# Moving the Fourier branch's gate projection beside attention in a two-layer hybrid block

## The chip, the cores and the metric

One Trainium2 chip, one core. The time is device microseconds (us) of one launch, taken as the median of the runs. The engines are TensorE (PE in the profile; PEld is its weight load), VectorE (DVE), ScalarE (ACT), GpSimd (POOL) and SyncE (SP), which issues all the transfers here. Each engine works through its own instructions in order.

## The reference

Two layers. Each normalises and modulates 1,024 latent tokens of width 1,024 (and in layer 0 a 256-token context prefix too), multiplies them by one wide matrix, and splits the columns over three branches, each multiplied by a SiLU gate before the output projection:

```python
hx = rms_norm(x, norm_g[l]) * (1.0 + scale[:, None, :]) + shift[:, None, :]
px = split_cols(hx @ w_in[l])         # q, k, v, g_att, c_a, c_b, g_conv, f_u, g_four
attn = windowed_attention(q, k, v, kc, vc, attn_sink[l])       # +-128 tokens, and the context
y_conv = conformer_conv(c_a, c_b, conv_w, conv_b, ln_g, ln_b)  # GLU, 31 taps, LayerNorm, swish
y_four = fourier_mix(f_u, w_four, b_four)                      # real part of a 2-D DFT, linear
y = jnp.concatenate([attn * silu(g_att), y_conv * silu(g_conv), y_four * silu(g_four)], -1)
x = x + gate[:, None, :] * (y @ w_out[l])
```

## The kernel before, in words

All is float32. Every large product is split into a high and a low part and done as three matmuls (`mm3`, lines 195 to 197). The unit of the work is a **block**: 128 columns of `w_in` against one chunk of tokens (`project`). A chunk is 512 latent tokens (128x512 matmuls) or the 256 context tokens (128x256); a block has 8 steps of depth, so 24 matmuls. The weights of the next 128 columns come by one transfer (`w_begin`, line 430) and are split into `wh` on ScalarE and `wl` on VectorE, or on GpSimd once attention runs (`split`, lines 404 and 405).

A layer has these stages:

1. The Fourier input columns, then the first GLU columns.
2. The list `todo` of column groups, which the generator `projections` walks block by block: the GLU columns (`C_A`, `C_B + P`, `C_A + P`), the Fourier gate (`C_GF`, two groups), keys, values, four groups of queries. In layer 0 a group is three blocks, in the last layer two, but three for keys and values. Between two blocks the loop takes one step of the generator `side`: the Fourier transform (`fourier`), then the output gate's sums (`gate_sums`, whose weight tiles are named `wada`, and whose last row is a small transfer from `b_ada` into the tile `gsum`), and in layer 0 the modulation of the next layer (`ada1`), four rounds of four 512 KB `wada` tiles in the same four buffers. A round's matmuls (line 285) read the buffers, and then the next round's transfers may be issued (line 276).
3. Attention: a pipeline of **steps**, four per 128 queries, 40 in layer 0 and 32 in the last. A step issues scores (lines 893, 895; tile `score`), transposes of the probabilities (949; `pt<-ident,p`) and products with the values (963; `mm<-ph,v` and `mm<-pl,v`), and after these **one block** of other work as filler: first the attention gate (`C_GATT`), then the convolution's gate (`C_GC`), then halves of the output projection (`Out.half`, also 24 matmuls), of which a tile of 128 tokens can have its two once its attention is done, stored to `od` and loaded again. A step without a filler has only its own matmuls.
4. The output halves that are left.

The depthwise convolution runs on VectorE: 31 **taps** per 128 channels and chunk group (`cy<-cu,cw,cy`), put into the queue `back` by `conv_taps` and taken out by `fill_v(us)`, some microseconds' worth per block by the table `budget`. The class `Behind` makes each wait, in the order of the program, behind VectorE's last instruction of other work. A scheduler then sets every engine's order at build time, by priority (the place in the program, lower first) and its own picture of time.

The Fourier gate's block ends with three operations: tanh on ScalarE, the gate `t<-t` on VectorE and the product with the branch `F<-F,t` on VectorE, and a store to `yd`:

```python
def g():
    V.scalar_tensor_tensor(out=th, in0=th, scalar=1.0, in1=o, op0=ALU.add, op1=ALU.mult)
def h():
    V.scalar_tensor_tensor(out=d, in0=d, scalar=scale, in1=th, op0=ALU.mult, op1=ALU.mult)
    nc.sync.dma_start(out=store[:, c0:c1], in_=d)
```

While attention runs, `g` is held to the start of the next step and `h` to its end.

Of the kernel before, what the change touches and what calls it, by code (L numbers as in the profile page):

```python
# [139 lines left out]
def tile_backbone(ctx: ExitStack, tc: tile.TileContext, a, out):  # L140
# [31 lines left out]

    def fill_v(us):
        V.background = True
        while back and us > 0:
            t, f = back.popleft()
            f()
            us -= t
        V.background = False


# [363 lines left out]
    def conv_taps(l, ct, u, z, spans):  # L545
# [7 lines left out]
        def tap(s0, s1, j):  # L553
# [3 lines left out]
                                   in1=z.cols(o0, o1), op0=ALU.mult, op1=ALU.add)  # L557
        for s0, s1 in spans:
            us = 1.25 if s0 == 0 else 0.4
            back.append((us, lambda a=(s0, s1): first(*a)))  # L560
            for j in range(KC):
                if j != 15:
                    back.append((us, lambda a=(s0, s1, j): tap(*a)))
        back.append((0.0, u.put))

# [601 lines left out]
    def drain(g):  # L1167
        for _ in g:
            pass
# [111 lines left out]
    for l in range(DEPTH):  # L1281
# [39 lines left out]
        def side():  # L1321

            yield from four
            tab.extend(bufs.get("rope") for _ in range(2))
            for i, name in enumerate(("k_cos", "k_sin")):
                nc.sync.dma_start(out=tab[i].lat, in_=a[name])
            gsum = bufs.get("gsum")
# [42 lines left out]
        def gf_evac(m):  # L1370
            def f(o, c0, c1):
                drain(four)
                gate_mul(F[m], 0.5, yd[256 + m * P:256 + (m + 1) * P, :])(o, c0, c1)
            return f, lambda: F[m].put()
# [3 lines left out]
        def values():  # L1378
# [5 lines left out]
            for g in range(0, NT, 4):  # L1384
# [18 lines left out]
                (C_A + P, full, glu_a(1, wctx), lambda: taps(1), mmx)]  # L1403
        for m in range(2):
            todo.append((C_GF + m * P, full) + gf_evac(m) + (mmx,))
        k_at = sum(len(t[1]) for t in todo) + 3
# [4 lines left out]
        q_at = sum(len(t[1]) for t in todo)  # L1411
        budget = [(3.0 if t[0] < C_V else 5.0) * (0.5 if c == 2 else 1.0) for t in todo for c in t[1]]
        for j in range(4):
# [3 lines left out]
        for i in range(q_at):  # L1417
            c = next(pj)
            steps(sd)
            if i >= k_at:  # L1420
                steps(kp)
# [20 lines left out]
        def rest():  # L1442
# [3 lines left out]
            for i, c in enumerate(pj):  # L1446
                if i == 4 * len(full) - 2:
                    raw = w_begin(l, C_GC)
                if i == 4 * len(full) - 1:
                    box.append(w_split(raw))  # L1450
# [201 lines left out]
```

## Time and profile before

| | |
|---|---|
| median of 3 runs | 1203.3 us (1202.12 to 1205.43) |
| the profiled execution | 1202.68 us, of which the span is 1200.6 us |
| TensorE busy | 1103.3 us (92%) |
| VectorE busy | 820.6 us (68%) |
| ScalarE, GpSimd busy | 554.7 us, 295.0 us |
| mean granted TensorE clock | 0.964 of 2.4 GHz |
| chain that ended last | PE 70%, DVE 10%, DMA 9%, ACT 4% |

The span is first to last instruction of the profiled execution; 2.1 us of its time lie around it. A view by windows adds up, for a stretch of the span, each engine's busy time and the number of its instructions, and gives the granted clock as a share of 2.4 GHz: 1.00 is all of the stretch at the upper level, 0.50 all of it at 1.2 GHz. The timeline gives an instruction's start, its duration, engine, line, output and inputs, and in brackets the idle time before it and what ended that. Matmuls overlap in it, so that a matmul's cost in a row of them is the distance between two starts.

### The profile page before, as it was taken

What the parts mean: (1) busy time and instruction counts of PE and PEld (TensorE: products, weight loads), DVE (VectorE), ACT (ScalarE), POOL (GpSimd) and SP (SyncE); (2) the same over time, 40 slices, a digit from 0 to 9 for tenths busy, and PEclk for the clock granted to TensorE, in tenths of its full rate; (3) what the DMA queues carried; (4) which work ended last, traced back from release to release, by engine and by line L of the source; (5) the groups of instructions that cost most, each with busy time, mean ns of one, the idle gap of its engine ahead of it and who ended that gap; (6) DMA issues with size and microseconds to landing.
All of it is one profiled execution on the core that took longest, in us unless ns stands there. A gap on an engine that the chain in (4) does not pass through costs nothing.

```text
span 1200.6 us, 17131 instructions
## 1 busy us (share of the span) xinstructions
PE 1103.3 (92%) x6165; PEld 925.9 (77%) x6165; DVE 820.6 (68%) x1665; ACT 554.7 (46%) x1209; POOL 295.0 (25%) x266
## 2 busy tenths in 40 slices
PE   5799999999999989999889999999989979988866
PEld 3488887888888878888668788788778868877754
DVE  3425879999577786666755369889656786766654
ACT  5563222312566655564646652222255654545541
POOL 1212000000222443544342120000022453334321
PEclk9799999999999999999979999999989989999889
DMA  9602273744332433544436423532243453322221
GB/s 332 218 25 71 70 239 113 225 137 108 84 97 75 149 115 102 166 142 132 115 120 227 145 65 116 184 110 79 88 93 106 136 145 103 110 74 71 71 71 53
DMA packets 154093, 146.49 MB, mean 122 GB/s; under 512 B 7398, under 2 KB 131734, under 8 KB 154008
## 3 DMA queue, kind: packets, MB, share of 16 engines
q1 hardware_dynamic: 154008, 145.40, 39.5%
q8 instruction: 49, 0.80, 0.3%
q14 instruction: 36, 0.29, 0.1%
HBM read 110.49 MB, written 34.87 MB: 121 GB/s over the span
## 4 chain that ended last, share of the span: by engine, by line
PE 70%; DVE 10%; DMA 9%; ACT 4%; issue 3%; SPq 2%; POOL 1%; DVEq 0%; ACTq 0%; POOLq 0%
PE mm L195 13%; PE mm L197 13%; PE mm L196 13%; PE pt L195 5%; PE pt L196 5%; PE pt L197 5%; PE mm L963 4%; PE pt L949 4%; DMA od<-ot 3%; PE score L893 2%; DVE score L57 2%; DVE pl L57 2%; PE score L895 2%; DMA wr<-od 1%; ACT p L919 1%
## 5 line engine op out<-in xcount | busy, mean ns | idle before, releaser
L195 PE MATMUL mm<-hxh,wh 128*128 128x512 f32 (+1 forms) x808 | 311.5, 386 | 5.5 <-DVE t L57 3.2
L197 PE MATMUL mm<-hxh,wl 128*128 128x512 f32 (+1 forms) x808 | 306.7, 380 | 2.4 <-POOL wl L405 2.3
L196 PE MATMUL mm<-hxl,wh 128*128 128x512 f32 (+1 forms) x808 | 307.4, 380 | 0.0
L195 PEld LDWEIGHTS mm<-hxh,wh 128*128 128x128 f32 x808 | 153.8, 190 | 37.5 <-DVE t L57 4.3
L57 DVE SCALAR_TENSOR_TENSOR cy<-cu,cw,cy 128x1014 f32<-128x1014 f32 (+20 forms) x180 | 180.1, 1007 | 2.6
L197 PEld LDWEIGHTS mm<-hxh,wl 128*128 128x128 f32 x808 | 153.6, 190 | 30.3 <-POOL wl L405 3.1
L935 POOL TENSOR_SCALAR p<-p,st 128x640 f32<-128x640 f32 (+2 forms) x144 | 114.4, 809 | 249.1 <-DVE st L57 129.1
L196 PEld LDWEIGHTS mm<-hxl,wh 128*128 128x128 f32 x808 | 154.0, 191 | 25.0 <-issue 0.5
L405 POOL TENSOR_TENSOR wl<-wr,wh 128x1024 fp32r<-128x1024 f32 x26 | 64.2, 2468 | 396.3 <-ACT wh L404 394.1
L954 ACT ACTIVATE ph<-pt 128x512 fp32r<-128x512 f32 x184 | 97.4, 542 | 121.0 <-PE pt L949 118.2
L57 DVE TENSOR_TENSOR pl<-pt,ph 128x512 fp32r<-128x512 f32 x184 | 112.3, 616 | 57.8 <-ACT ph L954 56.4
L949 PE MATMUL pt<-ident,p 128*128 128x128 f32 x640 | 107.6, 286 | 24.5 <-DVE pl L57 19.1
L919 ACT ACTIVATE p<-score,st 128x640 f32<-128x640 f32 (+2 forms) x144 | 105.3, 734 | 36.5 <-DVE st L57 29.2
L57 DVE CUSTOM_DVE_ANT_0 score<-score,mask,nsink 128x640 f32<-128x640 f32 (+2 forms) x144 | 110.8, 782 | 13.8 <-PE score L895 13.0
L195 PE MATMUL pt<-hxh,wh 128*128 128x512 f32 (+1 forms) x296 | 112.2, 383 | 3.9 <-ACT hxh L393 2.5
L404 ACT ACTIVATE wh<-wr 128x1024 fp32r<-128x1024 f32 x56 | 59.7, 1066 | 116.5 <-PE mm L196 73.1
L196 PE MATMUL pt<-hxl,wh 128*128 128x512 f32 (+1 forms) x296 | 111.1, 376 | 0.7 <-DVE hxl L57 0.7
L197 PE MATMUL pt<-hxh,wl 128*128 128x512 f32 (+1 forms) x296 | 110.4, 373 | 0.9 <-DVE wl L57 0.9
L949 PEld LDWEIGHTS pt<-ident,p 128*128 128x128 f32 x640 | 79.8, 146 | 38.2 <-POOL p L935 8.7
L963 PE MATMUL mm<-ph,v 128*128 128x256 f32 x320 | 93.1, 314 | 13.2 <-ACT ph L954 10.7
L963 PE MATMUL mm<-pl,v 128*128 128x256 f32 x320 | 93.7, 315 | 5.3 <-DVE pl L57 4.9
L963 PEld LDWEIGHTS mm<-ph,v 128*128 128x128 f32 x320 | 64.6, 202 | 18.3 <-ACT ph L954 15.8
(220 smaller groups left out, 1797.8 us busy)
## 6 DMA issues: line engine op xcount, KB each, us to landing
wada<-w_ada SPq DMA_DIRECT2D x48, 512.0 KB, 7.0
wr<-w_in SPq DMA_DIRECT2D x38, 512.0 KB, 4.1
qq<-qd SPq DMA_DIRECT2D x36, 256.0 KB, 4.3
x1d<-x SPq DMA_DIRECT2D x10, 512.0 KB, 3.0
xnd<-xr SPq DMA_DIRECT2D x10, 512.0 KB, 3.7
p<-xnd SPq DMA_DIRECT2D x10, 512.0 KB, 4.8
sg<-sgd SPq DMA_DIRECT2D x36, 128.0 KB, 3.0
od<-ot SPq DMA_DIRECT2D x18, 256.0 KB, 2.5
```

Source lines behind the costliest of these rows:

```text
L57: r = f(*args, **kw)
L195: T.matmul(o, lhsT=lhs[0], rhs=rhs[0], start=start, stop=False)
L196: T.matmul(o, lhsT=lhs[0], rhs=rhs[1], start=False, stop=False)
L197: T.matmul(o, lhsT=lhs[1], rhs=rhs[0], start=False, stop=stop)
L404: S.activation(hi, raw, AF.Copy)
L405: (E or (G if holding[0] else V)).tensor_tensor(out=lo, in0=raw, in1=f32(hi), op=ALU.subtract)
L893: T.matmul(sc[:, c0:512], lhsT=q2[:, h, :], rhs=kx[:, k0:k0 + nl], start=fst, stop=not fst)
L919: S.activation(pp[:, j * n:(j + 1) * n], z["sc"][j][:, 768 - n:768], AF.Exp, scale=-1.0, bias=st[:, j:j + 1], accum_out=st[:, 4 + j:5 + j])
L935: G.tensor_scalar(out=pp[:, j * n:(j + 1) * n], in0=pp[:, j * n:(j + 1) * n], scalar1=st[:, 6 + j:7 + j], scalar2=1.0, op0=ALU.mult, op1=A ...
L949: T.transpose(out=bt[:, (j % 2 * 2 + y) * P:(j % 2 * 2 + y + 1) * P], in_=pp[:, c0:c0 + P], identity=ident)
L954: S.activation(ph, bt[:, :w], AF.Copy)
L963: T.matmul(o, lhsT=self.vv[kt][:, kv * P:(kv + 1) * P], rhs=y.cols(j * 256, (j + 1) * 256), start=(j == 0 and x == 0), stop=(j == z["nkt"] ...
```

## The change

The Fourier gate's two column groups leave their place ahead of the keys and become the first fillers of attention (`q_at`, the number of blocks ahead of attention, falls by 6 in layer 0 and by 4 in the last). Their accumulators come from the two `mm` banks. What depended on the old place follows: the cosine and sine tables are loaded at the third block rather than behind the Fourier transform, `side` takes two steps per block from the first key block on, `budget` has 4 and 6 us instead of 3 and 5, and the convolution gate's weights are fetched two groups later. The taps get a priority later by 300, and the context's are put into the queue ahead of the latent's.

```diff
     def fill_v(us):
+        p0 = tc.cur_priority
+        tc.cur_priority = p0 + 300
         V.background = True
...
         V.background = False
+        tc.cur_priority = p0
...
-        for s0, s1 in spans:
+        for s0, s1 in spans[::-1]:
...
-        back.append((0.0, u.put))
+            back.append((0.0, u.put_ctx if s0 else u.put_lat))
...
             yield from four
-            tab.extend(bufs.get("rope") for _ in range(2))
-            for i, name in enumerate(("k_cos", "k_sin")):
-                nc.sync.dma_start(out=tab[i].lat, in_=a[name])
             gsum = bufs.get("gsum")
...
             def f(o, c0, c1):
-                drain(four)
                 gate_mul(F[m], 0.5, yd[256 + m * P:256 + (m + 1) * P, :])(o, c0, c1)
...
-        for m in range(2):
-            todo.append((C_GF + m * P, full) + gf_evac(m) + (mmx,))
         k_at = sum(len(t[1]) for t in todo) + 3
...
-        budget = [(3.0 if t[0] < C_V else 5.0) * (0.5 if c == 2 else 1.0) for t in todo for c in t[1]]
+        budget = [(4.0 if t[0] < C_V else 6.0) * (0.5 if c == 2 else 1.0) for t in todo for c in t[1]]
+        for m in range(2):
+            todo.append((C_GF + m * P, full) + gf_evac(m) + (mm,))
         for j in range(4):
             todo.append((C_GATT + j * P, full, gate_evac(sgd[j * P:(j + 1) * P, :]), None, mm))
...
             c = next(pj)
+            if i == 2:
+                tab.extend(bufs.get("rope") for _ in range(2))
+                for t, name in zip(tab, ("k_cos", "k_sin")):
+                    nc.sync.dma_start(out=t.lat, in_=a[name])
             steps(sd)
+            if i >= k_at - 3:
+                steps(sd)
             if i >= k_at:
...
-                if i == 4 * len(full) - 2:
+                if i == 6 * len(full) - 2:
                     raw = w_begin(l, C_GC)
-                if i == 4 * len(full) - 1:
+                if i == 6 * len(full) - 1:
                     box.append(w_split(raw))
```

Lines behind the first edit are 3 higher in the changed kernel (195 to 197 are 198 to 200). Three places of the built order:

**SP's queue, layer 0, ahead of attention**: the transfers of the last two rounds of `ada1` before (a round is four `wada` tiles; `wr` are weights of a column group, `qd<-q` stores queries).

```order
L276 DMA wada_1857<-w_ada 128x4x256
L276 DMA wada_1858<-w_ada 128x4x256
L276 DMA wada_1855<-w_ada 128x4x256
L276 DMA wada_1856<-w_ada 128x4x256
L430 DMA wr<-w_in 128x8x128
L1346 DMA qd_858<-q_150_2083 128x512
L276 DMA wada_1857<-w_ada 128x4x256
L276 DMA wada_1858<-w_ada 128x4x256
L276 DMA wada_1855<-w_ada 128x4x256
L276 DMA wada_1856<-w_ada 128x4x256
```

And now:

```order
L433 DMA wr<-w_in 128x8x128
L279 DMA wada_1738<-w_ada 128x4x256
L279 DMA wada_1739<-w_ada 128x4x256
L279 DMA wada_1736<-w_ada 128x4x256
L279 DMA wada_1737<-w_ada 128x4x256
L1346 DMA qd_858<-q_150_1878 128x512
L279 DMA wada_1738<-w_ada 128x4x256
L279 DMA wada_1739<-w_ada 128x4x256
L279 DMA wada_1736<-w_ada 128x4x256
L279 DMA wada_1737<-w_ada 128x4x256
L1346 DMA qd_858<-q_150_1878 128x512
```

The rounds stand closer: on TensorE the matmuls of one round and of the next had two blocks or three between them before, and have one now, which for the last round is a context block.

**VectorE's queue, layer 0, at the split `wl` of the first query group's weights** (`kr` is the key's rotation, `cy` the convolution's sums, of `cu` and the weights `cw`). Before, such a split stood so:

```order
L57 TENSOR_TENSOR kr_1762<-kr_1762,t_1811 128x512
L57 SCALAR_TENSOR_TENSOR cy_1352<-cu_1253,cw,cy_1352 128x1013
L57 SCALAR_TENSOR_TENSOR cy_1001<-cu_896,cw,cy_1001 128x243
L57 TENSOR_TENSOR wl<-wr,wh 128x1024
L57 SCALAR_TENSOR_TENSOR cy_1352<-cu_1253,cw,cy_1352 128x1014
```

And now:

```order
L57 SCALAR_TENSOR_TENSOR cy_1384<-cu_1283,cw,cy_1384 128x255 x2
L57 SCALAR_TENSOR_TENSOR cy_1384<-cu_1283,cw,cy_1384 128x254
L57 SCALAR_TENSOR_TENSOR cy_1384<-cu_1283,cw,cy_1384 128x253
L57 SCALAR_TENSOR_TENSOR cy_1384<-cu_1283,cw,cy_1384 128x252
L57 SCALAR_TENSOR_TENSOR cy_1384<-cu_1283,cw,cy_1384 128x251
L57 SCALAR_TENSOR_TENSOR cy_1384<-cu_1283,cw,cy_1384 128x250
L57 SCALAR_TENSOR_TENSOR cy_1384<-cu_1283,cw,cy_1384 128x249
L57 SCALAR_TENSOR_TENSOR cy_1384<-cu_1283,cw,cy_1384 128x248
L57 SCALAR_TENSOR_TENSOR cy_1384<-cu_1283,cw,cy_1384 128x247
L57 SCALAR_TENSOR_TENSOR cy_1384<-cu_1283,cw,cy_1384 128x246
L57 TENSOR_TENSOR wl<-wr,wh 128x1024
```

A run of 17 context taps now stands ahead of this split. In all, every tap of both layers still stands ahead of VectorE's third operation on attention scores.

**TensorE's queue, last layer, late in attention**. Before, a step had no filler between its two groups of scores and its products:

```order
L893 MATMUL score<-kh_7639,q_528_9846 128x384
L893 MATMUL score<-kd_7637,q_528_9846 128x384
L895 MATMUL score<-kh_7640,q_528_9846 128x256
L895 MATMUL score<-kd_7638,q_528_9846 128x256
L949 MATMUL pt<-ident,p_9952 128x128 x4
L963 MATMUL mm<-pl_9971,v_7873 128x256
L893 MATMUL score<-kh_7639,q_528_9846 128x384
L893 MATMUL score<-kd_7637,q_528_9846 128x384
```

The step before this one in the changed kernel's order ends with matmuls of an output half between the transposes and the next scores:

```order
L952 MATMUL pt<-ident,p_9730 128x128 x2
L198 MATMUL mm<-hxh_6194,wh 128x512
L199 MATMUL mm<-hxl_6196,wh 128x512
L200 MATMUL mm<-hxh_6194,wl 128x512
L198 MATMUL mm<-hxh_6198,wh 128x512
L199 MATMUL mm<-hxl_6200,wh 128x512
L200 MATMUL mm<-hxh_6198,wl 128x512
L896 MATMUL score<-kh_7447,q_528_9692 128x384
```

Of the last layer's 13 steps ahead of its last one, 6 had a block in the order before and 10 have one now; the order of the first 18 steps holds 15 blocks in both, and behind the last scores there are 4 in both. In layer 0 each of the last nine pairs or single steps of attention has at least one block now, where several had none.

## Rows read from the trace of the kernel before

**Rows 1.** The page: busy time of each engine, share of the span, instructions.
```profile
PE 1103.3 (92%) x6165; PEld 925.9 (77%) x6165; DVE 820.6 (68%) x1665; ACT 554.7 (46%) x1209; POOL 295.0 (25%) x266
```

**Rows 2.** Windows by stage: length, busy PE, PEld, DVE, ACT, POOL, clock, DMA, GB/s.
```profile
118.70:302.30 183.60, 183.60 (x1099) 150.86 (x1098) 164.66 (x251) 45.85 (x87) 2.95 (x1) 1.00 0.49 149
540.40:617.30 76.90, 70.64 (x383) 59.89 (x382) 49.35 (x149) 39.20 (x108) 32.73 (x36) 0.93 0.38 119
617.30:690.00 72.70, 65.79 (x310) 53.62 (x309) 34.39 (x85) 46.26 (x100) 20.77 (x21) 0.91 0.53 180
720.00:861.30 141.30, 141.24 (x709) 114.24 (x707) 119.84 (x141) 34.45 (x60) 0.15 (x1) 1.00 0.36 114
957.50:1008.00 50.50, 39.88 (x217) 34.70 (x216) 36.79 (x68) 24.48 (x55) 23.25 (x18) 0.93 0.50 144
1008.00:1043.90 35.90, 35.90 (x210) 31.63 (x209) 24.84 (x64) 18.41 (x45) 13.85 (x13) 1.00 0.29 96
1043.90:1149.10 105.20, 88.96 (x504) 76.33 (x502) 71.11 (x178) 58.23 (x139) 39.02 (x34) 0.94 0.25 70
```

**Rows 3.** Windows, line 195 alone (8 matmuls per block): PE, PEld.
```profile
540.40:617.30 76.90, 22.46 (x56) 10.66 (x56) 0.93 0.38 119
1008.00:1043.90 35.90, 12.63 (x32) 6.01 (x32) 1.00 0.29 96
1043.90:1149.10 105.20, 20.61 (x48) 9.76 (x48) 0.94 0.25 70
```

**Rows 4.** Timeline of PE: starts inside a latent block, then inside a context block.
```profile
299.65 0.39 PE L195 MATMUL mm<-hxh,wh 128*128 128x512 f32 x1
300.33 0.39 PE L195 MATMUL mm<-hxh,wh 128*128 128x512 f32 x1
...
176.32 0.28 PE L195 MATMUL mm<-hxh,wh 128*128 128x256 f32 x1
176.44 0.28 PE L196 MATMUL mm<-hxl,wh 128*128 128x256 f32 x1
```

**Rows 5.** Timeline of DVE: a Fourier gate's two operations, taps, a split, a wait.
```profile
167.28 0.69 DVE L57 SCALAR_TENSOR_TENSOR t<-t,pt 128x512 f32<-128x512 f32 x1 [1.79 <-ACT t L514]
168.01 0.69 DVE L57 SCALAR_TENSOR_TENSOR F<-F,t 128x512 f32<-128x512 f32 x1
168.62 5.21 DVE L57 SCALAR_TENSOR_TENSOR cy<-cu,cw,cy 128x1017 f32<-128x1017 f32 x4
...
187.91 4.56 DVE L57 SCALAR_TENSOR_TENSOR cy<-cu,cw,cy 128x243 f32<-128x243 f32 x9
...
215.25 1.22 DVE L57 TENSOR_TENSOR wl<-wr,wh 128x1024 fp32r<-128x1024 f32 x1
...
861.27 1.28 DVE L57 TENSOR_TENSOR cy<-cy,mm 128x512 f32<-128x512 f32 x2 [8.39 <-PE mm L576]
```

**Rows 6.** Timelines of PE and SP: one round of `ada1`, its buffers' reload; landings of `wada`.
```profile
230.39 1.07 PE L285 MATMUL mm<-wada,s2p 128*32 128x256 f32 x16
231.27 1.05 PE L285 MATMUL pt<-wada,s2p 128*32 128x256 f32 x16
...
231.09 2.62 SPq L276 DMA_DIRECT2D wada<-w_ada  x4
...
DMA to landing us min/median/max: 3.5/6.5/9.8
```

**Rows 7.** The tile `gsum` (ns, shortest/median/longest); a short store's landing among the DMA issues.
```profile
L339 ACT ACTIVATE gsum<-pt x8: 375/385/387, 176.0 to 785.3; 128x256 f32<-128x256 f32 x8
...
yd<-F SPq DMA_DIRECT2D x1, 256.0 KB, 2.0
```

**Rows 8.** Windows of 30 us: columns as in rows 2.
```profile
360.00:390.00 30.00, 28.40 (x176) 25.15 (x175) 21.41 (x51) 20.82 (x50) 8.72 (x9) 1.00 0.24 75
600.00:630.00 30.00, 24.40 (x107) 18.67 (x106) 17.79 (x51) 14.43 (x41) 14.92 (x17) 0.78 0.36 118
```

**Rows 9.** The chain that ended last, end of layer 0's attention: start, us, what.
```profile
633.29 5.23 DMA od<-ot
```

## The prediction

> **What bounds the kernel now.** The page first: TensorE is busy 92% of the span, VectorE 68% [rows 1]. All the products stay, so the change can only pay by what TensorE idles or runs at the lower clock. The windows by stage say where that is [rows 2]. From the first tap of layer 0 to the first attention scores (118.7 to 302.3) TensorE has not one idle microsecond and clock 1.00; in the last layer, from about the first tap to the convolution's mean (720 to 861.3), 0.06 us. Idle time is inside and behind attention. The yardstick there is 1008 to 1043.9: four steps with one block each (32 matmuls of line 195, 8 per block [rows 3]), TensorE full, 8.97 us per step. A block is 24 matmuls of 0.68 / 3 us = 5.44 us [rows 4], so the step's own matmuls are 3.53 us.
>
> Against that, 1043.9 to 1149.1 holds 13 steps and 48 / 8 = 6 blocks [rows 3], that is 13 x 3.53 + 6 x 5.44 = 78.5 us of work in 105.2 us: **a hole of 26.7 us**, 16.2 us of it idle and the rest slow matmuls (clock 0.94). Seven of these steps have no block, so a step without one costs 3.8 us beyond its work. At the end of layer 0 (540.4 to 690) 6.3 + 6.9 us are idle; the clocks 0.93 and 0.91 mean 2 x 0.07 x 76.9 + 2 x 0.09 x 72.7 = 23.9 us at 1.2 GHz; what of that is not idle (10.7 us) ran at half speed and lost 5.3 us: **a hole of 18.5 us**. These steps want for filler. The steps ahead of attention want for nothing, and from there the change takes its filler.
>
> **The parts.** *Moved blocks.* Layer 0: four latent blocks (5.44 us) and two context blocks (24 x 0.12 = 2.88 us [rows 4]), 27.5 us; last layer: four, 21.8 us. The stretches ahead of attention shrink on TensorE from 183.6 to 156.1 us and from 141.3 to 119.5 us. In attention the same 49.3 us return, and lengthen it only as far as they find no hole.
>
> *VectorE ahead of attention.* It was the cover's weak side: 164.7 us busy in 183.6, 119.8 in 141.3 [rows 2]. What leaves it: per latent block the pair gate and product, 168.62 - 167.28 = 1.34 us [rows 5] (a context block's pair taken as 0.75 us, by its half width with the fixed part), and two weight splits of 1.22 us per layer, which GpSimd does in attention. That leaves 164.7 - 5.4 - 1.5 - 2.4 = 155.4 us and 119.8 - 5.4 - 2.4 = 112.0 us: VectorE's work now fills the shorter stretch of layer 0 to 99%. If it never waits, the loss is 0. If it idles as long as before, layer 0's stretch is 155.4 + 18.9 = 174.3 us, 18.2 us more than TensorE's; in the last layer 21.5 us were idle, of which 8.4 us stood behind the last tap, waiting for TensorE [rows 5], so 112.0 + 13.1 - 119.5 = 5.6 us. Loss ahead of attention: **0 to 24 us**.
>
> Where in it? I can name three waits of layer 0 in the new order. (a) Reload of `ada1`: transfers are issued from 0.7 us after a round's first matmul, over 2.6 us, and land 6.5 us after issue in the middle of all, 3.5 to 9.8 us at the ends [rows 6]. The next round now starts after its own 1.9 us and one block: 7.3 us, and needs its last two tiles at 8.2 and 8.7 us; issued at 2.0 and 2.7 us they land at 8.5 and 9.2 us. About 1 us (with what rides on the queue between) for two rounds; behind the context block the round starts at 4.8 us and its second tile lands at 1.3 + 6.5 = 7.8 us where it is wanted at 5.3, so 2.5 us. Sum 4.5 us; with landings of 3.5 us nothing, with 9.8 us 13 us. (b) The bias of the gate's sums: ScalarE's 0.385 us, issue 0.25 us and a landing of at least 2.0 us [rows 7] against five matmuls (1.1 us) in the order: 1.5 us. (c) The split of the first query weights behind 17 context taps of 4.56 / 9 = 0.51 us [rows 5]: up to 8.6 us; I take 4, the middle. Layer 0 loses 10 us. The last layer has no `ada1` and every tap ahead of the mean: I take 3 us, the middle of 0 to 5.6. **Loss 13 us.**
>
> The Trainium skill (DMA: Bandwidth & Descriptors, Specifications) gives a first byte after 0.6 us and about 358 GB/s from HBM, from which I estimate 0.6 + 2.1 MB / 358 GB/s = 6.5 us for all four tiles. By it a reload would be complete 7.2 us after its round began, (a) would be 2 us, and the sum 2.5 us better. The landings of rows 6 are later than that, and the sum goes by them.
>
> *Attention, last layer.* Order: those 13 steps now carry 10 blocks, three carry none, and what lies around them holds as many blocks as before. Three steps at 3.8 us leave 11.4 us of the 26.7: **gain 15 us**, between 0 (the holes only move) and 26.7 us. *Layer 0*: blocks now stand in all the late steps; I take two thirds of 18.5 us, since a tail of transfers stays behind the last step (od<-ot 5.2 us [rows 9]): **12 us**, between 0 and 18.5. Other holes, as the one of 957.5 to 1008, where the output weights are split, move four steps on and keep their size.
>
> *The rest* I cost at nothing. The taps' later priority and the context-first order change who goes first on VectorE, not its sum, which stands above. The two splits per layer on GpSimd lie in 25% busy time [rows 1]; uncovered, 4 x 2.5 us. The column loads, the stores to `yd` and the tables are moved on SP past key and query stores; transfers fill 0.49 and 0.36 of their stretches [rows 2]. The held gate and product add 1.34 us of VectorE per filled step, 6 or 4 steps, where it has a third of its time idle.
>
> **Sum.** 1202.7 (the profiled execution, 0.6 us under the median) + 13 - 15 - 12 = 1188.7: **1189 us**. What follows last in these stretches is then VectorE ahead of attention and TensorE in it.
>
> **Rivals.**
> *A, the cover holds.* TensorE finds splits and reloads in time, since VectorE's taps start earlier (budget 4 and 6), and lone steps without a block cost little. Loss 0, gain 30 of 45: 1173 us. For it: VectorE's sum still fits, if barely. Against: a queue 99% full that also waits for TensorE's products.
> *B, the holes are not for want of filler.* Late steps wait for a round trip of attention to memory (5.2 us out [rows 9]), and more filler meets the same waits: gain halves to 13.5, equal to the loss: 1202 us. For: those transfers are on the chain. Against: four filled steps in a row show no wait at all.
> *C, VectorE starves TensorE ahead of attention, and the clock falls there.* Loss at its upper end, 24 us, in gaps. How gaps count: 1.6 us idle in 30 left the clock at 1.00, 5.6 us brought it to 0.78 [rows 8]; at the end of layer 0 the lower level lasted 23.9 / 13.2 = 1.8 times the idle time. 24 us idle then mean 43 us at 1.2 GHz, 19 of them busy, 9.6 us lost. 1202.7 + 24 + 9.6 - 27 = 1209 us. It decides from a loss above 27 + 3.6 = 31 us on. The Trainium skill (TensorE: Matmul & The Clock Gate, What's actually happening) has the lower clock as the default that activity releases, which speaks for C wherever waits come in clusters; the trace agrees at 0.78 and 1.00. For C: two stretches that were without a gap get a full VectorE. Against: waits (a) to (c) are 1 to 4 us apart by blocks of 5 us, like the harmless ones of 360 to 390.
>
> **Chances.** Forecast (1180 to 1198) 0.54; A 0.17; B 0.14; C 0.15. Three runs tell 0.3%, 3.6 us, from no change: faster is the forecast and A, 0.71; same is B, 0.14; slower is C, 0.15. The range leaves out about the far half of A and of C: 1172 to 1208. The forecast's own is 1180 to 1198.
>
> **What would show it.** Right: ahead of attention, idle time of TensorE ended by `wada` transfers, `gsum` and VectorE's splits, some 10 us in layer 0 and 3 in the last, clock near 1.00; first scores of layer 0 at about 285; in the last layer the 13 late steps with 80 matmuls of the first of the three lines in some 112 us. Wrong: no idle time there (A), as many holes in the late steps with blocks in them (B), or a clock below 0.95 ahead of attention (C).

## The result and the profile after

| | before | with the change |
|---|---|---|
| median of 18 runs each | 1202.49 us (1198.24 to 1206.85) | 1209.71 us (1204.73 to 1218.13) |
| ratio | | **1.0063**, 95% interval 1.0045 to 1.0081 |
| profiled execution | 1202.68 us | 1206.9 us (span 1204.9) |

The change made the kernel slower by 0.6%; 1189 had been forecast. On the page the engines look as in [rows 1]:

```profile
PE 1104.7 (92%) x6165; PEld 924.3 (77%) x6165; DVE 824.1 (68%) x1661; ACT 555.8 (46%) x1209; POOL 299.4 (25%) x270
```

The windows by stage of the changed kernel (columns as in [rows 2]) say more. From the first matmul on the tile `wf` in layer 0 to the first scores, the next eight steps, the end of layer 0, the hole of the last layer, and its late steps:

```profile
93.78:285.68 191.90, 182.95 (x1080) 147.24 (x1078) 156.44 (x244) 46.34 (x85) 1.21 (x3) 0.98 0.44 133
285.68:361.50 75.82, 69.80 (x420) 60.91 (x421) 54.85 (x118) 41.49 (x100) 18.31 (x19) 0.95 0.27 75
...
524.40:715.03 190.63, 183.03 (x963) 156.38 (x961) 115.82 (x306) 110.93 (x255) 82.12 (x78) 0.98 0.54 169
...
987.50:1052.50 65.00, 52.92 (x263) 44.97 (x262) 40.58 (x78) 28.81 (x65) 24.22 (x21) 0.87 0.42 118
1052.50:1152.40 99.90, 93.29 (x539) 81.03 (x537) 73.45 (x191) 56.25 (x132) 39.16 (x34) 0.98 0.30 95
```

TensorE had no idle time ahead of layer 0's attention before; now 9.0 us lie there and 6.0 in the next eight steps. The late steps are filled as forecast: the window of the last 13, for line 198 (195 before) alone, has 80 matmuls in 109 us (80 in 112 had been expected), where [rows 3] have 48.

```profile
1043.30:1152.40 109.10, 32.19 (x80) 15.22 (x80) 0.98 0.31 99
```

For the account below the program is cut at places that all versions have: the first matmul on `wf` in each layer, and steps counted by eight score matmuls each, 0 to 35 in layer 0 and 36 to 67 in the last. From each piece's time I take the blocks that the change put into it (24 matmuls: 5.44 us, context 2.88 us [rows 4]):

| piece | before, us | after, us | blocks moved, us | net |
|---|---|---|---|---|
| start to `wf` of layer 0 | 96.1 | 93.8 | 0 | -2.4 |
| to step 8 | 272.1 | 267.7 | -27.5 (six) | **+23.1** |
| steps 8 to 26 | 163.2 | 162.9 | -5.1 (two become context blocks) | +4.8 |
| step 26 to `wf` of the last layer | 173.2 | 190.6 | +32.6 (six) | **-15.2** |
| to step 36 | 172.8 | 154.5 | -21.8 (four) | +3.5 |
| steps 36 to 55 | 169.2 | 183.0 | +5.4 (one) | **+8.4** |
| step 55 to the end | 154.0 | 152.4 | +16.3 (three) | **-17.9** |

The sum is +4.3, the spans' 1204.9 - 1200.6. The first line is chance: it lies between 93 and 98 us in all the profiles. So the filler did find its holes, 33 us of them, and 40 us were lost. Three places stand out.

**First place: a bias behind key loads.** In the waits of the changed kernel from 150 to 305 us (engine, tile and line, what was waited for: us in total, times, longest) the bias of the gate's sums stands first:

```profile
PE pt L361 <- DMA gsum<-b_ada: 5.3, 1, 5.3
PE mm L198 <- DVE t L57: 4.3, 1, 4.3
PE mm L288 <- DMA wada<-w_ada: 2.8, 4, 1.4
```

The timelines of SP (its DMA issues) and of TensorE show why:

```profile
183.85 1.93 SPq L1357 DMA_DIRECT2D kd<-kd  x2
185.88 1.08 SPq L279 DMA_DIRECT2D wada<-w_ada  x2
187.49 1.09 SPq L1357 DMA_DIRECT2D kd<-kd  x2
188.62 0.44 SPq L349 DMA_DIRECT2D gsum<-b_ada  x1
...
192.72 2.04 PE L361 MATMUL pt<-gsum,sel 128*128 128x512 f32 x2 [5.32 <-DMA gsum<-b_ada]
```

And the window around it:

```profile
183.78:203.78 20.00, 14.68 (x56) 8.64 (x56) 13.49 (x21) 5.57 (x10) 0.00 (x0) 0.83 0.55 145
```

The last sums are written at 186.1 + 0.4 us; the transfer is issued 2.1 us later, behind two key loads, and lands 4.1 us after issue. The granted clock of these 20 us is 0.83: 2 x 0.17 x 20 = 6.8 us at 1.2 GHz.

**Second place: attention's start.** VectorE, GpSimd and TensorE around the first scores (285.68):

```profile
284.40 1.22 DVE L57 TENSOR_TENSOR q<-qq,q 64x1024 fp32r<-64x1024 f32 x1 [1.76 <-ACT q L870]
285.65 3.43 DVE L57 SCALAR_TENSOR_TENSOR cy<-cu,cw,cy 128x1010 f32<-128x1010 f32 x1
289.01 0.71 DVE L57 STREAM_SHUFFLE t<-q 128x512 f32<-128x512 f32 x1
289.63 0.27 DVE L57 TENSOR_TENSOR v<-pt,v 128x128 fp32r<-128x128 f32 x1
289.82 0.74 DVE L57 CUSTOM_DVE_ANT_0 score<-score,mask,nsink 128x512 f32<-128x512 f32 x1
290.49 0.68 DVE L57 SCALAR_TENSOR_TENSOR t<-t,mm 128x512 f32<-128x512 f32 x1
...
285.65 2.37 POOL L408 TENSOR_TENSOR wl<-wr,wh 128x1024 fp32r<-128x1024 f32 x1 [190.69 <-DVE q L57]
...
291.22 0.80 PE L198 MATMUL mm<-hxh,wh 128*128 128x512 f32 x1 [4.33 <-DVE t L57]
```

The first Fourier-gate block's accumulator is free only when VectorE has done its gate `t<-t,mm` at 290.49. Ahead of that stand a left-over tap and late operations of the last queries and values. The tap takes 3.43 us, where its neighbours take 1.27: GpSimd's split began in the same instant. From 283.78 to 303.78 the clock is 0.83 again.

**Third place: where the output weights are split** (the hole of 957.5 to 1008 before [rows 2], four steps later now). Here GpSimd and VectorE share the splits:

```profile
984.30 4.82 POOL L408 TENSOR_TENSOR hxl<-wor,hxh 128x512 fp32r<-128x512 f32 x3
...
983.34 0.41 DVE L57 CAST hxh<-wor 128x512 fp32r<-128x512 f32 x1
984.80 1.51 DVE L57 CAST hxh<-wor 128x512 fp32r<-128x512 f32 x1
986.34 0.42 DVE L57 TENSOR_TENSOR pl<-pt,ph 128x256 fp32r<-128x256 f32 x1
987.92 1.49 DVE L57 CAST hxh<-wor 128x512 fp32r<-128x512 f32 x1
989.32 0.88 DVE L57 CUSTOM_DVE_ANT_0 score<-score,mask,nsink 128x640 f32<-128x640 f32 x1
...
990.29 0.79 ACT L922 ACTIVATE p<-score,st 128x640 f32<-128x640 f32 x1 [4.60 <-DVE st L57]
...
991.23 0.69 PE L896 MATMUL score<-kh,q 128*128 128x384 f32 x1 [2.98 <-ACT p L922]
```

A cast of 0.41 us takes 1.5 beside GpSimd's three splits, so the maximum of the scores, the exponentials and the next scores come late one after the other.

### The profile page after: what moved, and what is told of

Its sections match the earlier page's. It is cut to its first block, busy times and chain, and to the rows that moved or that the text cites. A ratio compares the mean times of both kernels' runs of the same rounds, so it can differ in the third digit from the quotient of the medians.

```text
span 1204.9 us, 17143 instructions
## 1 busy us (share of the span) xinstructions
PE 1104.7 (92%) x6165; PEld 924.3 (77%) x6165; DVE 824.1 (68%) x1661; ACT 555.8 (46%) x1209; POOL 299.4 (25%) x270
## 4 chain that ended last, share of the span: by engine, by line
PE 64%; DMA 12%; DVE 12%; issue 4%; ACT 3%; SPq 3%; POOL 1%; DVEq 0%; ACTq 0%; POOLq 0%
PE mm L198 11%; PE mm L199 11%; PE mm L200 11%; PE pt L199 4%; PE pt L198 4%; PE pt L200 4%; PE mm L966 4%; PE pt L952 4%; DMA wada<-w_ada 2%; PE score L896 2%; DMA wr<-od 2%; DVE score L57 2%; PE score L898 2%; DVE cy L57 1%; DVE pl L57 1%
## 5 line engine op out<-in xcount | busy, mean ns | idle before, releaser
L198 PE MATMUL mm<-hxh,wh 128*128 128x512 f32 (+1 forms) x832 | 320.0, 385 | 15.7 <-DVE t L57 11.3
L199 PE MATMUL mm<-hxl,wh 128*128 128x512 f32 (+1 forms) x832 | 315.8, 380 | 0.0
L200 PE MATMUL mm<-hxh,wl 128*128 128x512 f32 (+1 forms) x832 | 314.6, 378 | 0.0
L198 PEld LDWEIGHTS mm<-hxh,wh 128*128 128x128 f32 x832 | 159.7, 192 | 47.0 <-DVE t L57 13.4
L57 DVE SCALAR_TENSOR_TENSOR cy<-cu,cw,cy 128x1009 f32<-128x1009 f32 (+23 forms) x180 | 179.8, 1018 | 2.0
L200 PEld LDWEIGHTS mm<-hxh,wl 128*128 128x128 f32 x832 | 159.1, 191 | 28.7 <-issue 1.1
L199 PEld LDWEIGHTS mm<-hxl,wh 128*128 128x128 f32 x832 | 159.7, 192 | 26.0 <-issue 1.5
L408 POOL TENSOR_TENSOR wl<-wr,wh 128x1024 fp32r<-128x1024 f32 x30 | 71.8, 2394 | 380.5 <-DVE q L57 190.7
L57 DVE CUSTOM_DVE_ANT_0 score<-score,mask,nsink 128x640 f32<-128x640 f32 (+2 forms) x144 | 111.8, 782 | 16.2 <-PE score L898 13.9
L198 PE MATMUL pt<-hxh,wh 128*128 128x512 f32 (+1 forms) x272 | 106.5, 395 | 2.2 <-ACT wh L407 1.9
L199 PE MATMUL pt<-hxl,wh 128*128 128x512 f32 (+1 forms) x272 | 103.7, 382 | 0.7 <-DVE hxl L57 0.7
L200 PE MATMUL pt<-hxh,wl 128*128 128x512 f32 (+1 forms) x272 | 103.3, 380 | 0.9 <-DVE wl L57 0.9
```

The costliest lines, as they stand in the source:

```text
L57: r = f(*args, **kw)
L198: T.matmul(o, lhsT=lhs[0], rhs=rhs[0], start=start, stop=False)
L199: T.matmul(o, lhsT=lhs[0], rhs=rhs[1], start=False, stop=False)
L200: T.matmul(o, lhsT=lhs[1], rhs=rhs[0], start=False, stop=stop)
L408: (E or (G if holding[0] else V)).tensor_tensor(out=lo, in0=raw, in1=f32(hi), op=ALU.subtract)
```

## The experiments

A ratio is to the kernel before, on the same chip. **Loss** compares profiles by piece: every matmul gets as its work the distance to the next start that its form usually has (the 30th percentile over all traces; 0.23 us for 128x512, 0.12 for 128x256), and what a piece takes beyond its work is lost. One execution per kernel stands behind each line, while the runs of a kernel spread over some 3 to 15 us. e5, whose compute engines work in the change's order row for row, differs from it by up to 3.7 us in a piece, so differences below 4 us are not read.

| us lost | `wf` to step 0 | 0-8 | 8-26 | 26 to `wf` | to 36 | 36-55 | 55-end | median |
|---|---|---|---|---|---|---|---|---|
| before | 11.9 | 1.9 | 16.3 | 28.7 | 6.8 | 27.4 | 43.8 | 1202.5 |
| the change | 26.0 | 10.9 | 21.4 | 13.2 | 10.3 | 35.2 | 26.5 | 1209.7 |
| e1, blocks put back | 18.5 | 8.7 | 16.7 | 27.9 | 7.6 | 24.6 | 39.4 | 1206.6 |
| e2, sums apart | 16.1 | 3.1 | 20.2 | 11.3 | 9.8 | 35.0 | 27.0 | 1189.8 |
| e3, splits on VectorE | 27.1 | 8.8 | 19.4 | 12.5 | 12.2 | 29.6 | 20.1 | 1199.5 |
| e4, before with splits on VectorE | 11.9 | 2.3 | 26.1 | 32.0 | 7.9 | 30.3 | 33.0 | 1208.6 |
| e5, bias by ScalarE | 28.6 | 8.8 | 20.6 | 11.8 | 8.7 | 33.8 | 22.8 | 1206.3 |
| e6, e2 and e3 | 18.5 | 4.6 | 18.8 | 14.6 | 10.5 | 33.0 | 19.3 | 1183.8 |
| e7, old budget | 27.2 | 19.6 | 25.9 | 10.5 | 18.5 | 22.5 | 22.3 | 1210.1 |
| e8, other banks | 25.6 | 10.3 | 22.9 | 13.9 | 7.6 | 27.6 | 24.4 | 1198.5 |
| e9, output weights on GpSimd | 28.7 | 7.8 | 23.7 | 8.3 | 8.7 | 35.7 | 33.6 | 1213.5 |
| e10, e6 and e8 | 15.7 | 4.0 | 18.0 | 10.8 | 7.5 | 32.4 | 24.4 | 1186.6 |
| e11, no bias | 23.8 | 9.7 | 20.5 | 10.0 | 9.6 | 34.6 | 30.2 | 1200.5 |
| e12, fewer taps | 25.2 | 3.3 | 23.1 | 12.6 | 8.6 | 37.1 | 27.8 | 1204.4 |
| e13, output weights on VectorE | 26.7 | 10.8 | 23.2 | 8.2 | 10.0 | 29.0 | 22.0 | 1197.9 |
| e14, e6 and e13 | 16.2 | 4.5 | 18.0 | 13.7 | 10.4 | 30.4 | 22.9 | 1182.6 |
| e15, before with e3 and e13 | 11.9 | 2.7 | 23.6 | 30.7 | 7.8 | 27.1 | 33.2 | 1202.2 |

### The move or its companions (e1, e7)

e1 puts the blocks back and keeps the other edits:

```diff
+        for m in range(2):
+            todo.append((C_GF + m * P, full) + gf_evac(m) + (mmx,))
         k_at = sum(len(t[1]) for t in todo) + 3
...
-        for m in range(2):
-            todo.append((C_GF + m * P, full) + gf_evac(m) + (mm,))
```

> The changed kernel with the Fourier gate's blocks put back ahead of the keys; tap budgets, context taps first, double side steps and the tables' place are kept. Theory (the moved blocks cost more ahead of attention, some 18 us in layer 0 and 3 in the last, than they give back in it): the time is that of the kernel before, 1202.5 us within 3, and the last layer's late hole of 26.7 us is back. Rival 1 (the edits that go with the move, budget, order of taps and side steps, cost the 7 us): the time stays at 1209 to 1212 us or goes higher, since the gain in attention is lost too.

Measured: 1206.56 us, ratio 1.0035 (1.0021 to 1.0050), between the two. The late holes are back (39.4 lost), but ahead of step 8 it loses 27.2 us, where before 13.8. So the companions (steps of `side` in pairs, tap budget, context taps first) cost ahead of attention by themselves: 13 of the 23 us by which the change loses more there than the kernel before, though not in the same waits (no wait for the bias, but four for `wada`, 3.3 us in all). No run leaves out the pairs of `side` steps alone. Attention's start has the same wait as in the change (PE, then VectorE):

```profile
315.36 0.80 PE L198 MATMUL mm<-hxh,wh 128*128 128x512 f32 x1 [4.46 <-DVE t L57]
...
313.36 1.22 DVE L57 TENSOR_TENSOR q<-qq,q 64x1024 fp32r<-64x1024 f32 x1 [3.23 <-ACT q L870]
```

No tap is in the way here: VectorE itself idles 3.23 us in front of the gate, in its fixed order, for later queries.

e7 changes the numbers of `budget` in the change back to 3.0 and 5.0.

> The changed kernel with the taps' budget of before, 3 and 5 us per block instead of 4 and 6. Theory (VectorE's backlog at attention's start costs, and a smaller budget makes it longer): 1 to 10 us slower than the change, 1211 to 1220, with longer waits for VectorE at the start of attention. Rival (taps in the way of splits ahead of attention are what costs): 3 to 8 us faster, 1202 to 1206.

Measured: 1210.1 us, 1.0065 (1.0044 to 1.0087): no different from the change. By pieces it loses 10 us more ahead of step 8 and 8 more in the last layer's stretch, as the theory had it, and 13 less in steps 36 to 55, which nobody had. That the two cancel is chance.

### The bias (e2, e5, e11)

e2 puts four more steps of `side` between the sums and their use. As these steps go in pairs there, that is two more blocks, not four as its expectation has it; the rounds of `ada1` come later by as much:

```diff
             yield from gate_sums(l, gsum.lat)
-            yield
+            for _ in range(5):
+                yield
```

> The changed kernel with four more blocks between the gate's sums and their use in layer 0 and the last, so that the transfer of the bias (which the profile shows waited for, 5.32 us) has time to land. Theory: this wait and the half clock behind it (some 2 us) are part of the loss ahead of attention; the time falls by 5 to 7 us to about 1203, first scores of layer 0 at about 279 us instead of 285.7. Rival 2 (VectorE is what fills the stretch ahead of attention, so that TensorE would wait for VectorE instead): the time falls by less than 2 us, first scores stay at about 284 to 286, and the idle time appears behind VectorE.

Measured: **1189.75 us, 0.9892 (0.9860 to 0.9923)**, 20 us below the change, three times what was expected. First scores come at 278.1. The pieces to step 8 lose 17.7 us less; the rest is as in the change. The wait for the bias is gone, and so is the one of 4.33 us at attention's start: the build also ordered that place otherwise (the scores of step 1 follow those of step 0, with no block between). At least two repairs in one edit, so they had to be told apart.

e5 keeps the order of TensorE, VectorE, ScalarE and GpSimd row for row:

```diff
-        nc.sync.dma_start(out=gsum[2:3, :], in_=a["b_ada"]...)
+        nc.scalar.dma_start(out=gsum[2:3, :], in_=a["b_ada"]...)
```

> The changed kernel with one edit: the bias of the gate's sums is sent from ScalarE's queue instead of SP's, where it stood behind key loads; TensorE's and VectorE's orders are the same row for row. Theory (of the 20 us that the run with the sums set apart gave, about half belongs to this wait with its half clock, 5.3 + 3 us, and the other half, the wait of 4.33 us at attention's start, is its consequence, because VectorE idled meanwhile and carries its taps into attention): the time falls by 12 to 20 us to 1190 to 1198, and the wait of 4.33 us is gone or below 1.5. Rival 4 (the two losses are separate, the second comes from the order at attention's start): it falls by 5 to 9 us, and the wait of 4 us stays. Rival 5 (the transfer engines are full at that time, so that the bias lands as late from any queue): less than 2 us.

Measured: 1206.25 us, 1.0035 (1.0015 to 1.0055). The transfer in the view of the tile `gsum` (issue time in ns, first and last start in us):

```profile
L349 ACTq DMA_DIRECT2D gsum<-b_ada x1: 509/509/509, 186.8 to 186.8; - x1
```

The matmul that waits for it, in the timeline:

```profile
192.15 1.98 PE L361 MATMUL pt<-gsum,sel 128*128 128x512 f32 x2 [4.51 <-DMA gsum<-b_ada]
```

And the window up to its issue:

```profile
176.80:186.80 10.00, 9.60 (x69) 6.04 (x68) 9.66 (x11) 2.10 (x4) 0.00 (x0) 1.00 1.09 348
```

Issued at once, at 186.8, it lands 5.3 us later instead of 4.1: 4 KB wait among weights and keys that fill the transfer engines (DMA share 1.09). That is rival 5 for the mechanism; the median is 3.5 us lower, with intervals that overlap. It is the moment that is wrong, not the queue.

e11 leaves the bias transfer out.

> The changed kernel without the transfer of the gate's bias (the bias is left out of the output gate), so that nothing waits for it; TensorE's order is the change's through layer 0's start of attention and on to its middle. This isolates the wait of 5.32 us. Theory (the wait and the lower clock behind it cost 8 to 10 us, and the loss at attention's start, 9 us more than before, is another place): 1198 to 1203, first scores of layer 0 at about 277, and still a wait for VectorE of 3 us or more at attention's start. Rival (the second loss follows from the first, through taps that VectorE puts off while it idles): 1188 to 1194, and no such wait. Rival 5b (the stretch ahead of attention is full for VectorE or the transfers anyway, and another wait takes its place): 1206 or more.

Measured: 1200.46 us, 0.9993 (0.9976 to 1.0009), 9 us below the change by the medians, 8 by the ratios, as the theory had it. TensorE's order is the change's up to 469 us, so the cost can be read at its place. The same three matmuls in the change, the first ahead of the wait, the second behind it and the third behind the last round of `ada1`:

```profile
172.49 1.07 PE L288 MATMUL pt<-wada,s2p 128*32 128x256 f32 x16
203.86 0.68 PE L198 MATMUL mm<-hxh,wh 128*128 128x256 f32 x1
240.50 0.95 PE L303 MATMUL pt<-sel,t 128*128 128x2 f32 x8
```

And in e11:

```profile
174.17 1.07 PE L288 MATMUL pt<-wada,s2p 128*32 128x256 f32 x16
197.25 0.68 PE L198 MATMUL mm<-hxh,wh 128*128 128x256 f32 x1
240.03 0.95 PE L303 MATMUL pt<-sel,t 128*128 128x2 f32 x8
```

From the first to the second it takes 31.4 us with the wait and 23.1 without: **the wait of 5.32 us costs 8.3 us where it stands**, 3.0 of them by slower matmuls behind it. But from the first to the third only 2.1 us are left. The other 6.1 go to waits that were shorter or absent in the change, and to the clock. The waits of line 288 from 150 us on, and a window of e11:

```profile
PE mm L288 <- DMA wada<-w_ada: 2.5, 5, 0.7
PE pt L288 <- DMA wada<-w_ada: 1.6, 2, 0.9
PE pt L288 <- ACT vr L531: 1.4, 1, 1.4
...
223.78:243.78 20.00, 17.94 (x106) 13.03 (x105) 13.81 (x26) 2.76 (x5) 0.00 (x0) 0.83 0.44 145
```

So first scores were missed (285.2; 277 expected), and other waits took the place of the first, as rival 5b had it. The profiled execution, 1203.36 us, is 2.9 us above its kernel's median, and the change's is 2.8 below; why the medians lie further apart than the traces no trace shows. The waits from 150 us on still begin with `PE mm L198 <- DVE t`, 4.35 us at attention's start: the second place is a loss of its own.

### Attention's start (e8, e12)

e8, from the same banks as ahead of attention:

```diff
-            todo.append((C_GF + m * P, full) + gf_evac(m) + (mm,))
+            todo.append((C_GF + m * P, full) + gf_evac(m) + ((mm if m else mmx),))
```

> The changed kernel with one edit: the first group of the Fourier gate takes its accumulators in turn from both kinds of banks, as the blocks ahead of attention do, instead of from the two mm banks alone. Up to attention's first scores TensorE's order stays as it is (one small matmul apart), the wait for the gate's bias among it; behind them the scores of step 1 follow those of step 0 with no block between, as in the run with the sums set apart. Theory (the wait of 4.33 us at attention's start, with the half clock behind it, comes from this order and is a loss of its own): 5 to 10 us faster than the change, 1200 to 1205, with no wait over 1.5 us between first scores and step 1. Rival 4b (VectorE is behind at that point, whatever the order, and TensorE waits for it a little later): 1207 to 1211, with a wait of 3 us or more for VectorE in the first eight steps.

Measured: 1198.52 us, 0.9982 (0.9964 to 1.0000). The time met the theory and the trace refuted it. Steps 0 to 8 lose 10.3 us, as in the change; TensorE now waits a little later:

```profile
299.05 0.58 PE L896 MATMUL score<-kh,q 128*128 128x256 f32 x1 [3.29 <-ACT p L922]
```

The gain lies in steps 36 to 55 of the last layer, 7.6 us, which the edit wasn't aimed at. There the third place is smaller: steps 50 to 52 take 31.3 us in the change (first line) and 20.2 in e8 (second line), though e8 moves no split.

```profile
987.50:1018.78 31.28, 21.91 (x102) 17.94 (x100) 21.69 (x38) 15.20 (x31) 14.16 (x11) 0.86 0.49 135
988.71:1008.86 20.15, 18.60 (x107) 15.87 (x105) 15.69 (x32) 11.56 (x26) 13.13 (x10) 1.00 0.63 181
```

e12 leaves eight taps per layer out:

```diff
-                if j != 15:
+                if j != 15 and not (ct and j > 22 and s0 == 0):
```

> The changed kernel without the last eight latent taps of the second channel group, in both layers (they are left out of the convolution, 8 x 1.2 us of VectorE per layer, which stand around the first scores). Theory (VectorE, with taps left over at attention's start, is what TensorE waits for there): the first eight steps of layer 0 lose 3 to 5 us instead of 10.9, the stretch ahead of the last layer's attention some 3 us less than 10.3, and the time falls by 8 to 12 us to 1198 to 1202. Rival (the wait comes from the order at the start, as in the run with the blocks put back, where VectorE idled and TensorE waited 4.5 us all the same): less than 4 us, 1206 to 1210.

Measured: 1204.37 us, 1.0022 (1.0001 to 1.0044). Steps 0 to 8 lose 3.3 us instead of 10.9. Of its waits from 150 us on, the bias still costs its share and the start next to nothing:

```profile
PE pt L361 <- DMA gsum<-b_ada: 6.1, 1, 6.1
...
PE mm L198 <- DVE t L57: 0.5, 1, 0.5
```

So in the change's order the left-over taps are the second loss: 5 us by the medians, 7.6 by the piece. e1 shows that the place can be lost to another order too.

### Splits on GpSimd (e3, e4, e6, e9, e10, e13 to e15)

e3 and e4 change `(E or (G if holding[0] else V))` in `split` to `(E or V)`, in the changed kernel and in the one before. Both expectations give a wrong number of splits: 18 and 10 are those beside which a VectorE instruction was stretched; there are 30 and 26 (`wl<-wr,wh` on GpSimd: 71.8 us in x30 with the change).

> The changed kernel with the 18 weight splits of attention on VectorE (1.22 us each by the rows of other splits) instead of GpSimd (2.37 us each). Theory (a split on GpSimd stretches the VectorE instruction beside it, 23.4 us in 18 splits, 1.3 us each, so it is no free cover): VectorE loses 22 us of work and gains 23 back; the time changes by less than 3 us, the stretched instructions of VectorE beside splits are gone, and the wait of 4.33 us at the start of attention shrinks. Rival 3 (the stretch is chance, splits on GpSimd are free): VectorE's busy time rises by 22 us and the time by 3 to 8 us.

> The kernel before with its 10 splits of attention on VectorE. Theory: 17.9 us of stretched instructions go, 12.2 us of splits come; the time is the same within 2 us or up to 3 us lower. Rival 3 (splits on GpSimd are free): 2 to 5 us slower.

Measured: e3 1199.50 us, 0.9970 (0.9954 to 0.9986), 10 us below the change; e4 1208.57 us, 1.0050 (1.0035 to 1.0065), 6 us above the kernel before. The same edit has both signs. e3 gains in steps 36 to 55 and behind (5.6 and 6.4 us), with VectorE 9.2 us busier:

```profile
PE 1098.9 (92%) x6165; PEld 919.2 (77%) x6165; DVE 833.3 (70%) x1691; ACT 555.8 (47%) x1209; POOL 237.8 (20%) x240
```

e6 joins e2 and e3.

> The changed kernel with the gate's sums apart and the 18 splits of attention on VectorE. Theory (the two repair different places, the start of layer 0's attention and the hole where the output weights are split): 1189.7 - 8 = 1182 us within 4. Rival 6 (the 10 us of the splits came from the same place, attention's start): 1188 to 1195.

Measured: **1183.80 us, 0.9856 (0.9837 to 0.9875)**; 4 us short of the sum of the two gains, 1179.5. e10 adds e8's edit to e6.

> The changed kernel with three edits together: the gate's sums apart, the splits of attention on VectorE, and the first Fourier-gate group's accumulators from both kinds of banks. Theory (the third edit gains in the last layer, 9 us by its rows of the stretch ahead of the output halves, and that is a place of its own): 1174 to 1181. Rival 8 (the gains of these edits are orders that happen to be better than the change's, and don't add): 1182 to 1190.

Measured: 1186.59 us, 0.9879 (0.9847 to 0.9912): rival 8, e8's gain doesn't carry over.

For the third place, e9 and e13 move the output weights' splits to one engine:

```diff
-            split(self.hi[k].lat[:, hs], self.lo[k].lat[:, hs], self.raw[h, k], V if k % 2 else G, k % 2 == 1)
+            split(self.hi[k].lat[:, hs], self.lo[k].lat[:, hs], self.raw[h, k], G, k % 2 == 1)
```

> The changed kernel with all low parts of the output weights split on GpSimd, where VectorE did every other one. Theory (the holes of steps 16 to 26 in layer 0 and 50 to 55 in the last, 17 and 21 us in the change against 10 and 15 before, are VectorE's: splits stand ahead of the products' low parts pl, for which TensorE waits): the two holes shrink by 5 to 12 us together and the time falls to 1198 to 1205. Rival 7 (GpSimd, busier, stretches VectorE's instructions as much as the splits it takes over): 1207 to 1212.

Measured: 1213.47 us, 1.0109 (1.0083 to 1.0135): rival 7. With GpSimd doing all of them, the hole stays (35.7 us lost in steps 36 to 55). e13 has `V` for `G` in that line.

> The changed kernel with all low parts of the output weights split on VectorE, so that GpSimd has none of them (in the change it does every other one: three of them together, 4.82 us at 984.30, lie beside VectorE casts of 1.5 us where 0.58 is the median, and TensorE waits 2.98 us at 991.23). Theory (the holes at these splits come from VectorE and GpSimd stretching one another): the holes of steps 16 to 26 in layer 0 and 50 to 55 in the last, 17 and 21 us in the change, shrink by 5 to 12 us together, and the time falls by 4 to 10 us to 1200 to 1206. Rival 9 (VectorE's sum of work in those steps is what counts, and 16 more splits of 0.7 us lengthen it): 1209 to 1216.

Measured: 1197.89 us, 0.9971 (0.9952 to 0.9990), 12 us below the change though VectorE does more. Steps 36 to 55 lose 29.0 instead of 35.2, near the 27.4 of before; steps 8 to 26 don't improve. As e7 and e8 shrink the same piece by 12.7 and 7.6 us with these splits untouched, e13 supports the theory and doesn't prove it. e14 is e6 with this edit, e15 the kernel before with both.

> The changed kernel with the gate's sums apart and all splits, of attention's weights and of the output's, on VectorE. Theory: 1183.8 less 3 to 8 us, 1175 to 1181. Rival 9: 1184 to 1192.

> The kernel before with all these splits on VectorE. Theory: 2 to 6 us below its run with attention's splits alone there (1208.6), 1202 to 1207. Rival 9: 1208 to 1216.

Measured: e14 **1182.58 us, 0.9831 (0.9801 to 0.9860)**, between theory and rival and not told apart from e6; e15 1202.15 us, 0.9996 (0.9978 to 1.0013), 6 us below e4 and equal to the kernel before. With none of these splits on GpSimd in either kernel, the change with the sums apart is worth 1.6% (0.9831 to 0.9996; 1.3 to 2.0% with the two intervals joined).

## Why the prediction was wrong

The step that failed is the loss. The sum had 13 us of it, all ahead of attention; the table of pieces has 40, of which 26.6 lie ahead of attention or at its start (23.1 in layer 0, 3.5 in the last) and 13.2 in two pieces that were costed at nothing. The gain, 27 forecast, was 33. Term by term:

- **The gain in the late steps** was right: 12 and 15 us forecast, 15.2 and 17.9 by the table of pieces; the filler and its 80 matmuls stand where they were said to.
- **The last layer ahead of attention**: 3 forecast, 3.5, which agrees but is less than one execution can show.
- **(b), the bias: the largest mis-sized term.** It was 1.5 us, with a landing of 2.0 us taken from a lone store [rows 7]. The wait is 5.32 us and costs 8.3 where it stands (e11). Two things were missing: that the new order (the move and the pairs of `side` steps together; no run tells them apart) puts this transfer into the very microseconds in which keys and `wada` fill the transfer engines, and the clock, 0.83 around the wait. The order of SP's queue was at hand and showed the key loads ahead of it.
- **(c)** was too large: for the split behind the context taps TensorE didn't wait. **(a)** looks too large, with two waits of `ada1`, 2.0 us together, where 4.5 had been forecast (the other two waits for `wada` are the gate sums' own). But the wait of (b) gave the reloads time: without the bias (e11) the reloads wait some 3.5 us, and the clock falls. The two terms were added as if they were independent.
- **Attention's start was not in the sum.** The overfull VectorE queue (99%) was seen, but the loss was looked for only ahead of the first scores. It came behind them: taps left over, 7.6 us by e12.
- **"Other holes ... move four steps on and keep their size"** failed: +8.4 us in steps 36 to 55. GpSimd's splits stretch VectorE's casts there, and e13, without them on GpSimd, takes 6 us back; but e7 and e8 take back more by another order alone. So the cause of this loss is argued and not shown, and the +4.8 us of steps 8 to 26 are open.
- **"The two splits per layer on GpSimd lie in 25% busy time" and cost nothing** failed. They stop VectorE (below): the first of them stretched the tap at attention's start by 2.16 us. What the two cost in time no run tells apart.
- **The taps' later priority** was said to change who goes first. It changes nothing: the built orders of all five engines are the same without it.
- **Rival C** gave 1209 us and the time is its time, but not by its mechanism alone. Loss ahead of and at the start (+23.1) and the lower clock are its; that VectorE starves TensorE holds for the second place only, and the first is a transfer. With a gain 6 us above that of its sum, meeting the number is in part luck.

With the sums set apart (e2) the kernel stands at 1189.75, the number forecast; that is no confirmation, since late gains and a better start there pay for holes that had grown.

## What to carry to other kernels

When blocks are moved away from small transfers, ask for each what now shares its moment, not only what lies ahead in its queue: here 4 KB cost 8.3 us, and in the run with two blocks more between (e2) nothing waited for them. Terms that wait on the same stretch of the queue don't add: take one away and the next shows. Filler moved behind a full VectorE queue takes the queue's tail along, so look for the loss at the first steps after the move. And an edit that re-lays a scheduler's order moves holes elsewhere by some 5 to 13 us (e7, e8): test a cause by its place in the trace, not by the total.

## What was not expected of the hardware

Some instructions of VectorE that start while GpSimd works on a split stand still until it ends. The tap at 285.65 took 3.43 us beside a split of 2.37, its neighbours 1.27 (2.16 more). It reads two operands from the on-chip memory SBUF, as the sums of the softmax, `st<-st`, do, which were stretched all eight times in this trace. Casts of `wor`, with one input, were stretched too. But 57 instructions that have an accumulator of TensorE among their operands started inside a split, and none took more than 0.01 us longer than usual: at 986.34, above, `pl<-pt,ph` takes 0.42 us while the casts around it take 1.5. Summed over the trace, VectorE's instructions took some 49 us beyond the median of their form beside GpSimd's work (those over it by more than 0.3 us); 39 to 45 before, by how forms are grouped, and 21 in e14, where nearly all that is left lies beside other work of GpSimd. The Trainium skill (SBUF — State Buffer, SBUF: two separate sides) has it: VectorE and GpSimd share a port pair, and whichever starts first holds it for a whole instruction while the other blocks; of VectorE only instructions with two SBUF inputs, or in a mode that takes two ports, are concerned. The trace agrees, for the stretched and for the untouched ones. By that rule a split on GpSimd should not have been costed at nothing while VectorE has taps left.

Around one wait of 5.3 us the granted clock was 0.83 in the 20 us shown, and the wait cost 8.3 us at its place, where 1.6 us of idle time in 30 had left the clock at 1.00 [rows 8].

A transfer of 4 KB landed 4.1 us after its issue in one queue and 5.3 in another, with the transfer engines' share at 1.02 (183.78 to 193.78, the change) and 1.09 (e5): a queue of its own did not help here, where the engines behind the queues were full.
